# Keeping the split second expert matrix in a DRAM scratch between passes

## The chip, the cores and the metric

The kernel runs on one core of a Trainium2 chip. The metric is the device time of one execution, in microseconds (us). The kernel before takes 5032.78 us, the median of 3 runs (5029.45 to 5037.81).

## What is computed

The reference is two layers of a token mixer followed by an expert layer. The mixers and norms don't matter here. The expert layer does, cut to its core:

```python
def peer(h, wq, subkeys, u, v):
    # expert [t, heads, 16] and gate [t, heads, 16] come from a product-key search
    a = gelu(einsum('cd,chkd->chk', h, u[expert]))
    w = gate * a
    return einsum('chk,chkd->cd', w, v[expert])
```

There are 16384 experts of 1024 numbers each. Layer 0 works on 512 latent and 256 context tokens, layer 1 on the 512 latent ones. Everything is float32.

## The kernel before, in words

**Tiles and passes.** Tokens stand in tiles of 128. The second sum is computed as a dense product over all 16384 experts: a table `P` holds, for a pair of token tiles, the summed factor of each expert, and `vpass` (line 1027) multiplies it by the whole matrix `peer_v`. One call of `vpass` is a pass. Layer 0 has three passes, for the tile pairs (2,3), (4,5) and (0,1); layer 1 has two, for (2,3) and (0,1). So `peer_v` of a layer is read three times or twice.

**Columns.** A pass walks 128 columns `j`, in two halves of 64. Column `j` is the 128 x 1024 block of the experts `i*128 + j`, 512 KB. `load(jj)` (line 1033) fetches it on SP's queue (line 1042) into a float32 tile, ScalarE copies it into a float16 tile (line 1043), and the remainder is computed by VectorE (line 1045) or GpSimd (line 1047), so that `vh` holds a high and a low float16 part, again 512 KB. In the first pass of a layer a quarter of the remainders goes to VectorE, in the later passes half of them. TensorE then does 12 matmuls of 512 columns (line 1060). The tiles have names: the source is `s4` (three buffers) and `vh` is `hl` (three buffers), but each fourth column uses `h2Uh` and `h2Ul`, with one buffer each.

**What runs beside it.** During a half of a pass, `Scatter.step` (line 1147) builds the next table: per step four comparisons and products on VectorE (lines 1167 to 1170), 16 matmuls of 64 columns (lines 1172 and 1173) and copies back. The second half of the last pass of a layer has no such work. For tiles marked dense, `Scatter.at` (line 1108) multiplies the table by values from a spill (line 1120) and splits it (lines 147 and 149) for TensorE. For the tiles that are not dense, `gather` (line 908) fetches one row of the first expert matrix per token with an indirect DMA on GpSimd's queue (line 920, 512 KB) and multiplies it on VectorE (line 926), 128 times for each tile, through three buffers `r`. Layer 0 has three such tiles, layer 1 one. `Scatter.prep` (line 1131) of a tile that is not dense first issues what is left of its gather.

**What sets the order.** The program emits the work of a column, then a rate of background steps (`tick`, with `RATES`). A planner then orders the instructions of each engine by when it expects them to be ready, with the order of emission as priority; it may move work forward across columns and passes. The engines follow that order. One order is written by hand: `queue_behind` (line 901) places each gather on GpSimd's queue behind `self.lo_ins`, the most recent remainder that was given to GpSimd (line 1047 or 161).

Of the kernel before, what the change touches and what calls it, by code (L numbers as in the profile page):

```python
# [9 lines left out]
F16 = mybir.dt.float16  # L10
# [39 lines left out]
class Hybrid:  # L50
# [17 lines left out]
            for l in range(layers):  # L68
                self.layer(l, last=l == 1)

    # ---------------------------------------------------------------- constants
    def consts(self):
        nc, c, tmp = self.nc, self.cst, self.tmp
        dl = tmp.tile([128, 128], F32, name="dl")
# [37 lines left out]
                gens.pop(0)  # L112

    def tick(self, gens, rate):
        """Moves the generators on by rate on the average."""
        self.due = getattr(self, "due", {})
        k = id(gens)
        self.due[k] = self.due.get(k, 0.0) + rate
        n = int(self.due[k])
        self.due[k] -= n  # L120
        self.step(gens, n)
# [54 lines left out]
        nc.tensor.matmul(out, al, bh, start=False, stop=stop)  # L176


    # ---------------------------------------------------------------- modulation
    def srow(self, src, which, dst=None):  # L180
        dst = src if dst is None else dst
        self.nc.scalar.dma_start(src, self.i["cvec"][which].partition_broadcast(128))
# [28 lines left out]


    def vectors(self, l, last, pool, ps):
        """The factors that vary along a row, written out as rows."""
        nc = self.nc
        n = 4 if last else 8
        c = pool.tile([128, 8, KC], F32, name="vcol", bufs=1)
        md = self.modT[l]
        for w in range(n // 4):
            nc.vector.tensor_scalar(c[:, w * 4], md[2][:, :, w], 1.0 / WS, None, op0=OP.mult)  # L220
            nc.vector.scalar_tensor_tensor(c[:, w * 4 + 1], md[4][:, :, w], 1.0, self.g2[l], op0=OP.add, op1=OP.mult)
            nc.vector.tensor_copy(c[:, w * 4 + 2], md[3][:, :, w])
            nc.vector.tensor_scalar(c[:, w * 4 + 3], md[5][:, :, w], 1.0 / PS, None, op0=OP.mult)
        nc.tensor.transpose(ps[:n * KC, :128], c[:, :n].rearrange("p r k -> p (r k)"), self.idf)
        r = pool.tile([64, 128], F32, name="vrow", bufs=1)
        nc.scalar.activation(r[:n * KC], ps[:n * KC, :128], AF.Copy)
        self.vec = self.tc.dram_tile([n, D], F32, name=f"vec{l}")
        nc.sync.dma_start(self.vec.rearrange("r (k c) -> (r k) c", c=128), r[:n * KC])
# [3 lines left out]
        self.nc.sync.dma_start(r, self.vec[which * 4 + k].partition_broadcast(128))  # L232
        return r

    # ---------------------------------------------------------------- layer
    def load_x(self, tile_, t, eng=None, c=0):
        e = eng or self.nc.sync
        if self.res is None:
# [31 lines left out]
            self.res = self.nxt  # L270
            self.lo_ins = None

    # ---------------------------------------------------------------- mixers
    def mixers(self, l, last, wes):
        tiles = XTILES if last else XTILES + CTILES
        qkv_es = ExitStack()
# [197 lines left out]
        self.split(nat[:, 0], nat[:, 1], self.roped(pr, p, pool, "r", k, 4))  # L474
        self.to_stack(self.rtT, pr, 0 if k == "q" else 2, nat, ps)

    # ---------------------------------------------------------------- attention
    def probs_T(self, ap_, ps, e, nk):
        nc = self.nc
        tp = ps.tile([128, D], F32, name="w2", bufs=2)  # L480
# [166 lines left out]


    def strips(self, l, h, pool):
        """Decay by distance: forwards over positive, backwards over negative distances, both at zero."""  # L650
        nc = self.nc
        if h == 0:
            lg = self.lg = pool.tile([128, 8], F32, name="lg", bufs=1)
            nc.sync.dma_start(lg, self.i["decay"][l].partition_broadcast(128))
            nc.scalar.activation(lg, lg, AF.Exp, scale=-1.0)
            nc.scalar.activation(lg, lg, AF.Ln, bias=1.0)
            self.ng = pool.tile([128, 3, 8], F32, name="ng", bufs=1)
            for x, f in enumerate((-1.0, -256.0, -512.0)):
                nc.vector.tensor_scalar(self.ng[:, x], lg, f, None, op0=OP.mult)
            self.dd = pool.tile([128, 896], F32, name="dd", bufs=1)  # L660
            nc.gpsimd.iota(self.dd, pattern=[[1, 896]], base=-384, channel_multiplier=-1,
                           allow_small_or_imprecise_dtypes=True)
        dd, lg, ng = self.dd, self.lg, self.ng
        f, b = h, 4 + h
        s = pool.tile([128, 896], F32, name="strip")
        w = pool.tile([128, 896], F32, name="stript", bufs=1)
        nc.vector.tensor_scalar(s, dd, lg[:, f:f + 1], 0.0, op0=OP.mult, op1=OP.max)
        nc.vector.tensor_scalar(w, dd, ng[:, 0, b:b + 1], 0.0, op0=OP.mult, op1=OP.max)
        nc.vector.tensor_tensor(s, s, w, op=OP.add)
        nc.scalar.activation(s, s, AF.Exp, scale=-1.0)  # L670
        nc.vector.scalar_tensor_tensor(s, dd, 0.0, s, op0=OP.is_equal, op1=OP.add)
        c = pool.tile([128, 640], F32, name="stripc", bufs=1)
        nc.scalar.activation(c, dd[:, 256:896], AF.Exp, scale=ng[:, 0, f:f + 1], bias=ng[:, 1, f:f + 1])
        nc.scalar.activation(w[:, :640], dd[:, 256:896], AF.Exp, scale=lg[:, b:b + 1], bias=ng[:, 2, b:b + 1])
        nc.vector.tensor_tensor(c, c, w[:, :640], op=OP.add)
        return s, c


    # ---------------------------------------------------------------- output projection, second norm
    def wload(self, l, es, c):  # L680
        nc = self.nc
        pool = self.pool(es, f"wow{c}", 1, side="right")
# [74 lines left out]
        for t in order[len(order) - WLAG:]:  # L757
            second(t)

    # ---------------------------------------------------------------- product-key routing  # L760
    def routing(self, l, pool, ps, tiles, rp):
        nc = self.nc
        n = len(tiles)
# [133 lines left out]
        self.rt[t] = (st.rearrange("p a k h -> p a (k h)"), sg.rearrange("p k h -> p (k h)"), ix)  # L897


    # ---------------------------------------------------------------- gathered first expert matrix  # L900
    def queue_behind(self, ins):
        if self.lo_ins is not None:
            self.tc.add_manual_dep(ins.ins, self.lo_ins.ins.name,
# [29 lines left out]
        yield  # L933


    # ---------------------------------------------------------------- experts
    def need(self, t):
        while t not in self.done:
            self.step(self.bg, 1)
# [1 line left out]
    def peer(self, es, l, last, h2s):  # L941
# [30 lines left out]
        with ExitStack() as e:  # L972
            ps = self.pool(e, "ups", 4, space=PSUM)
            self.upass(l, 1, sc, ps, "pa", RATES[l][1], PRATE[l], more)
        self.accp = self.pool(es, "acc", 1, space=PSUM)
        for n, tiles in enumerate(self.groups):
            if n == 2:
                r = lambda: self.gp.tile([128, D], F32, name="r")
                vec = [self.srow(r(), 0, self.hpp.tile([128, D], F32, name="hp")), self.srow(r(), 1)]
                self.rg.append(self.ada(1, range(6), vec, r, lambda: self.sp.tile([128, D], F16, name="gst", bufs=GST)))  # L980
            follow = Scatter(self, self.groups[n + 1]) if n + 1 < len(self.groups) else None
            self.vpass(l, tiles, int(tiles[0] > 3), sc, follow, RATES[l][2 + 2 * n:4 + 2 * n])
            sc = follow
# [43 lines left out]
    def vpass(self, l, tiles, which, sc, follow, rates):  # L1027
# [3 lines left out]
        for half in range(2):  # L1031
            ahead = sc.step(1) if half == 0 else follow.step(0) if follow else iter(())
            def load(jj):
                j = half * 64 + jj
                ws = sc.at(half, jj)
                if j % 4 == 3:
                    v = self.lp.tile([128, 1536], F32, name="h2Uh")[:, :D]
                    vh = self.lp.tile([128, 3072], F16, name="h2Ul")[:, :2 * D].rearrange("p (z d) -> p z d", z=2)
                else:
                    v = self.vp.tile([128, D], F32, name="s4", bufs=3)  # L1040
                    vh = self.vp.tile([128, 2, D], F16, name="hl", bufs=3)
                nc.sync.dma_start(v, vr[:, j])
                nc.scalar.activation(vh[:, 0], v, AF.Copy)  # L1043
                if j % 4 in VDVE[sum(sc.dense)]:
                    nc.vector.tensor_tensor(vh[:, 1], v, vh[:, 0], op=OP.subtract)  # L1045
                else:
                    self.lo_ins = nc.gpsimd.tensor_tensor(vh[:, 1], v, vh[:, 0], op=OP.subtract)  # L1047
                return ws, vh

            vs = [load(jj) for jj in range(PF[1])]  # L1050
            for jj in range(64):
                j = half * 64 + jj
                if jj + PF[1] < 64:
                    vs.append(load(jj + PF[1]))
                ws, vh = vs.pop(0)
                for s in range(2):
                    a, b = ws[s]
                    for i, (w, x) in enumerate(((a, 0), (a, 1), (b, 0))):
                        for hf in range(2):
                            nc.tensor.matmul(acc[s][hf], w, vh[:, x, hf * 512:hf * 512 + 512],  # L1060
                                             start=j == 0 and i == 0, stop=j == 127 and i == 2)
                if jj % 2 == 1:
                    next(ahead, None)
                self.tick(self.rg, 0.4)
                self.tick(self.bg, rates[half])
# [22 lines left out]


class Scatter:  # L1090
    """Sums the gates of a pair of tiles into a table over all experts; over given values the sums are multiplied in."""

    def __init__(self, o, tiles, G=False):
        self.o, self.tiles, self.G = o, tiles, G
# [2 lines left out]
        self.sT = {}  # L1097

    def col(self, half, jj, n=1):
        """The table's columns jj.. of a half."""  # L1100
        w = 32 if half else 64
        p = self.P[half][jj // w]
        return p[:, :, jj % w:jj % w + n] if n > 1 else p[:, :, jj % w]
# [2 lines left out]
        return p[:, s].rearrange("p j t -> p (j t)").bitcast(F16).rearrange("p (z j t) -> p z j t", z=2, t=128)  # L1106

    def at(self, half, jj):
        """The stationary operands of expert column jj: a pair of parts for each token tile."""
        o, nc = self.o, self.o.nc  # L1110
        x, w = jj % 2, 32 if half else 64
        if any(self.dense) and x == 0:
# [143 lines left out]
```

## Time and profile before

| what | value |
| --- | --- |
| median of 3 runs | 5032.78 us |
| span of the profiled execution | 5040.9 us |
| first pass of layer 0 (first to last matmul) | 1469.2 to 1977.0 us |
| second pass of layer 0 | 1989.6 to 2505.2 us |
| third pass of layer 0 | 2517.2 to 2912.1 us |
| first pass of layer 1 | 4143.2 to 4613.2 us |
| second pass of layer 1 | 4630.7 to 5023.2 us |
| TensorE, VectorE, ScalarE, GpSimd busy | 90%, 72%, 44%, 44% of the span |

The profile is of one execution, whose span is 8.1 us (0.16%) above the median of the runs shown. Busy shares are averages over stages with different limits, so the passes are read one by one, in windows that begin at the first matmul of line 1060 of a half pass and end with its last.

### The profile page before, as it was taken

To read this page: it belongs to the slowest core of one execution; us is meant where nothing else is said; L and a number is where in the kernel's file an instruction comes from. 1 tells how busy PE (TensorE), PEld (TensorE's weight loads), DVE (VectorE), ACT (ScalarE), POOL (GpSimd) and SP (SyncE) were. 2 spreads that over 40 slices of the span, in tenths; PEclk is the share of its full clock that TensorE was granted. 3 is DMA by queue.
4 is the path that set the end of the run, shared out by engine and by line. 5 is a ranking of instruction groups with operands and counts; after the bars stand their busy time and mean duration, and the time that the engine had idled before them with its cause. 6 is when DMAs were issued, how large, how long until landed. Compare 5 with 4: busy or idle time off the path is not lost. (4 is left out here: it accounts for less than half of the span.)

```text
span 5040.9 us, 79837 instructions
## 1 busy us (share of the span) xinstructions
PE 4516.0 (90%) x30416; PEld 2857.2 (57%) x30416; DVE 3624.2 (72%) x7163; ACT 2209.1 (44%) x3694; POOL 2221.1 (44%) x1493
## 2 busy tenths in 40 slices
PE   4987888978999988998899999788878999998998
PEld 3664566745665554554555467455545766655553
DVE  7777549897889999988798245745775777667543
ACT  5556344343433343433334466644444443343443
POOL 4224133457566665555233422422456544443333
PEclk9996999989999998999899999799999999998999
DMA  5421446668777767877578632144657764445555
GB/s 180 150 65 35 156 134 208 194 196 282 249 255 251 247 245 256 290 256 277 188 235 270 202 122 66 39 145 134 208 183 251 249 222 149 143 151 166 168 188 176
DMA packets 379873, 955.15 MB, mean 189 GB/s; under 512 B 43632, under 2 KB 158800, under 8 KB 379488
## 3 DMA queue, kind: packets, MB, share of 16 engines
q1 hardware_dynamic: 296000, 675.74, 41.6%
q0 software_dynamic: 73888, 268.53, 15.0%
q10 hardware_dynamic: 9600, 5.77, 0.4%
q8 instruction: 238, 3.90, 0.3%
q14 instruction: 147, 1.20, 0.1%
HBM read 920.49 MB, written 29.41 MB: 188 GB/s over the span
## 5 line engine op out<-in xcount | busy, mean ns | idle before, releaser
L1047 POOL TENSOR_TENSOR hl<-s,hl 128x1024 f16<-128x1024 f32 x384 | 861.8, 2244 | 1077.0 <-ACT hl L1043 1075.1
L1060 PE MATMUL acc<-hl,gst 128*128 128x512 f16 x3456 | 835.4, 391 | 17.6 <-DVE gst L149 9.0
L926 DVE SCALAR_TENSOR_TENSOR r<-r,hp 128x1024 f32<-128x1024 f32 x512 | 619.4, 1213 | 284.0 <-DMA r<-peer_u,ix 283.1
L1043 ACT ACTIVATE hl<-s 128x1024 f16<-128x1024 f32 x480 | 505.2, 1057 | 697.7 <-PE acc L1060 313.5
L1060 PEld LDWEIGHTS <-gst 128*128 128x128 f16 x4608 | 463.9, 101 | 565.6 <-issue 58.5
L920 POOL DMA_INDIRECT r<-peer_u,ix x512 | 547.2, 1069 | 391.5 <-DVE r L926 193.1
L1172 PE MATMUL pw<-oh,oi 128*128 128x64 f16 x2560 | 640.1, 300 | 72.0 <-DVE oh L1169 70.7
L1173 PE MATMUL pw<-ol,oi 128*128 128x64 f16 x2560 | 639.9, 301 | 13.7 <-DVE ol L1170 13.5
L1060 PE MATMUL acc<-hl,P 128*128 128x512 f16 x2304 | 558.5, 389 | 5.2 <-POOL hl L1047 3.1
L1060 PEld LDWEIGHTS <-P 128*128 128x128 f16 x3072 | 307.8, 100 | 354.1 <-issue 27.7
L1172 PEld LDWEIGHTS <-oi 128*128 128x128 f16 x2560 | 372.5, 146 | 133.9 <-DVE oh L1169 74.0
L174 PE MATMUL pw<-h2Uh,hl 128*128 128x384 f16 x1024 | 352.4, 344 | 56.4 <-ACT gst L1017 56.2
L1169 DVE TENSOR_TENSOR oh<-oj,sT 128x512 f16<-128x512 f16 x320 | 257.8, 806 | 201.8 <-PE pw L1172 197.5
L161 POOL TENSOR_TENSOR hl<-s,hl 128x1024 f16<-128x1024 f32 x136 | 299.0, 2200 | 227.0 <-ACT hl L160 173.3
L1173 PEld LDWEIGHTS <-oi 128*128 128x128 f16 x2560 | 373.4, 146 | 18.5 <-issue 1.5
L176 PE MATMUL pw<-h2Uh,hl 128*128 128x384 f16 x1024 | 351.8, 344 | 25.1 <-DVE hl L151 18.9
L176 PE MATMUL pa<-h2Uh,hl 128*128 128x384 f16 x1024 | 341.8, 334 | 34.7 <-POOL hl L161 34.6
L175 PE MATMUL pw<-h2Ul,hl 128*128 128x384 f16 x1024 | 351.7, 343 | 0.0
L174 PE MATMUL pa<-h2Uh,hl 128*128 128x384 f16 x1024 | 342.6, 335 | 1.5 <-ACT hl L160 1.5
L175 PE MATMUL pa<-h2Ul,hl 128*128 128x384 f16 x1024 | 341.1, 333 | 0.0
L176 PEld LDWEIGHTS <-hl 128*128 128x128 f16 x2048 | 207.0, 101 | 214.3 <-POOL hl L161 50.2
L1045 DVE TENSOR_TENSOR h2Ul<-h2Uh,h2Ul 128x1024 f16<-128x1024 f32 x160 | 233.6, 1460 | 130.3 <-ACT h2Ul L1043 130.3
(297 smaller groups left out, 9801.1 us busy)
## 6 DMA issues: line engine op xcount, KB each, us to landing
s<-peer_v SPq DMA_DIRECT2D x480, 512.0 KB
s<-ut SPq DMA_DIRECT2D x256, 512.0 KB
h2Uh<-peer_v SPq DMA_DIRECT2D x160, 512.0 KB
wq<-peer_wq SPq DMA_DIRECT2D x128, 256.0 KB
wst<-w_in SPq DMA_DIRECT2D x96, 256.0 KB
r<-w_ada SPq DMA_DIRECT2D x48, 512.0 KB
h2T<-w_ada SPq DMA_DIRECT2D x32, 512.0 KB
spill<-gst SPq DMA_DIRECT2D x64, 256.0 KB
```

The lines of the kernel that those rows point to most:

```text
L161: self.lo_ins = nc.gpsimd.tensor_tensor(lo, w, hi, op=OP.subtract)
L174: nc.tensor.matmul(out, ah, bh, start=start, stop=False)
L175: nc.tensor.matmul(out, ah, bl, start=False, stop=False)
L176: nc.tensor.matmul(out, al, bh, start=False, stop=stop)
L920: self.queue_behind(nc.gpsimd.indirect_dma_start(out=r, out_offset=None, in_=self.i["peer_u"], in_offset=bass.IndirectOffsetOnAxis(ap=ix[: ...
L926: nc.vector.scalar_tensor_tensor(r, r, 1.0, hp, op0=OP.mult, op1=OP.mult, accum_out=a[:, k - AHEAD:k - AHEAD + 1])
L1043: nc.scalar.activation(vh[:, 0], v, AF.Copy)
L1047: self.lo_ins = nc.gpsimd.tensor_tensor(vh[:, 1], v, vh[:, 0], op=OP.subtract)
L1060: nc.tensor.matmul(acc[s][hf], w, vh[:, x, hf * 512:hf * 512 + 512], start=j == 0 and i == 0, stop=j == 127 and i == 2)
L1169: nc.vector.tensor_tensor(oh, oj, col[2].to_broadcast([128, 64, TB]), op=OP.mult)
L1172: nc.tensor.matmul(pp[:, t0 - tb + x], oi[:, :, x], oh[:, :, x], start=True, stop=False)
L1173: nc.tensor.matmul(pp[:, t0 - tb + x], oi[:, :, x], ol[:, :, x], start=False, stop=True)
```

## The change

In the first pass of a layer each column's `vh` is stored to a DRAM scratch `vsplit`, on SP's queue, after the column's matmuls were emitted. In the later passes `load` fetches that block into a tile and does nothing else. These passes load three columns ahead of the matmuls in the order of emission instead of one, and use `s4`, `hl`, `h2Ul` and `h2Uh` as tiles for what they load. Comments that the diff also drops are left out here.

```diff
@@ peer
         self.accp = self.pool(es, "acc", 1, space=PSUM)
+        self.vsplit = self.tc.dram_tile([128, 128, 2, D], F16, name=f"vsplit{l}")
         for n, tiles in enumerate(self.groups):
+            self.first = n == 0
@@ vpass
             def load(jj):
                 j = half * 64 + jj
                 ws = sc.at(half, jj)
+                if not self.first:
+                    if j % 4 == 3:
+                        vh = self.lp.tile([128, 3072], F16, name="h2Ul" if j % 8 == 3 else "h2Uh")[:, :2 * D]
+                    else:
+                        vh = self.vp.tile([128, 2 * D], F16, name="s4" if j % 4 == 1 else "hl", bufs=3)
+                    vh = vh.rearrange("p (z d) -> p z d", z=2)
+                    nc.sync.dma_start(vh, self.vsplit[j])
+                    return ws, vh
...
-            vs = [load(jj) for jj in range(PF[1])]
+            pf = PF[1] if self.first else 3
+            vs = [load(jj) for jj in range(pf)]
             for jj in range(64):
                 j = half * 64 + jj
-                if jj + PF[1] < 64:
-                    vs.append(load(jj + PF[1]))
+                if jj + pf < 64:
+                    vs.append(load(jj + pf))
                 ws, vh = vs.pop(0)
...
+                if self.first:
+                    nc.sync.dma_start(self.vsplit[j], vh)
                 if jj % 2 == 1:
                     next(ahead, None)
```

## Rows read from the trace of the kernel before

**Rows 1.** Costliest groups of the page: busy us, mean ns | idle before, releaser.

```profile
L1047 POOL TENSOR_TENSOR hl<-s,hl 128x1024 f16<-128x1024 f32 x384 | 861.8, 2244 | 1077.0 <-ACT hl L1043 1075.1
...
L1043 ACT ACTIVATE hl<-s 128x1024 f16<-128x1024 f32 x480 | 505.2, 1057 | 697.7 <-PE acc L1060 313.5
...
L1045 DVE TENSOR_TENSOR h2Ul<-h2Uh,h2Ul 128x1024 f16<-128x1024 f32 x160 | 233.6, 1460 | 130.3 <-ACT h2Ul L1043 130.3
```

**Rows 2.** Windows: stretch, length, PE, PEld, DVE, ACT, POOL busy, PEclk, DMA share, GB/s.

```profile
1469.20:1709.70 240.50, 233.60 (x1250) 136.77 (x1251) 236.29 (x329) 83.83 (x95) 167.40 (x98) 0.97 0.70 244
1716.40:1977.00 260.60, 238.52 (x1269) 138.92 (x1270) 245.94 (x325) 99.92 (x127) 159.41 (x99) 0.95 0.70 241
1989.60:2228.70 239.10, 232.47 (x1233) 134.84 (x1233) 214.57 (x344) 94.17 (x156) 133.81 (x92) 0.96 0.82 283
2230.40:2505.20 274.80, 244.61 (x1274) 140.14 (x1273) 215.96 (x362) 96.76 (x129) 120.08 (x78) 0.91 0.67 230
2517.20:2744.40 227.20, 224.98 (x1234) 133.50 (x1234) 219.04 (x331) 83.07 (x125) 79.95 (x34) 0.99 0.77 258
2746.10:2912.10 166.00, 166.00 (x772) 75.43 (x771) 45.71 (x51) 67.90 (x72) 64.93 (x32) 1.00 0.65 204
4143.20:4369.50 226.30, 226.30 (x1250) 135.29 (x1251) 158.92 (x230) 83.81 (x95) 105.08 (x48) 0.99 0.47 149
4372.80:4613.20 240.40, 232.65 (x1269) 137.96 (x1270) 160.56 (x235) 99.24 (x125) 99.65 (x45) 0.98 0.48 154
4630.70:4855.50 224.80, 224.80 (x1218) 131.74 (x1219) 120.60 (x238) 98.10 (x152) 76.88 (x33) 0.97 0.54 173
4857.30:5023.20 165.90, 165.90 (x770) 75.05 (x767) 49.62 (x66) 73.36 (x92) 63.82 (x30) 1.00 0.63 197
```

**Rows 3.** Groups by line, second pass of layer 0 (1989 to 2505 us).

```profile
L926 DVE SCALAR_TENSOR_TENSOR r<-r,hp 128x1024 f32<-128x1024 f32 x105 | 127.3, 1213 | 62.2 <-DMA r<-peer_u,ix 62.0
```

**Rows 4.** Waits, 2230 to 2505 us: who waited for whom, us, times, longest.

```profile
DVE r L926 <- DMA r<-peer_u,ix: 38.3, 19, 4.8
...
PE acc L1060 <- DVE gst L149: 9.0, 2, 5.9
```

**Rows 5.** Windows of three other stretches, columns as in rows 2.

```profile
1139.00:1220.00 81.00, 61.70 (x343) 36.87 (x342) 64.42 (x95) 28.17 (x47) 56.64 (x43) 0.89 0.86 285
2380.00:2410.00 30.00, 23.44 (x96) 9.95 (x96) 19.25 (x32) 9.75 (x12) 16.96 (x13) 0.89 0.92 320
...
1469.00:1977.00 508.00, 474.34 (x2536) 277.72 (x2537) 485.90 (x662) 186.17 (x226) 329.46 (x199) 0.95 0.70 245
```

**Rows 6.** DMA of the first pass of layer 0 (1469 to 1977 us).

```profile
DMA packets 35448, 124.27 MB, mean 245 GB/s; under 512 B 3937, under 2 KB 5601, under 8 KB 35414
```

**Rows 7.** DMA of the first pass of layer 1 (4143 to 4613 us).

```profile
DMA packets 22917, 71.16 MB, mean 151 GB/s; under 512 B 2545, under 2 KB 6641, under 8 KB 22886
```

**Rows 8.** Groups by line, 1139 to 1220 us, where gathers stand closest.

```profile
L926 DVE SCALAR_TENSOR_TENSOR r<-r,hp 128x1024 f32<-128x1024 f32 x30 | 36.3, 1215 | 16.7 <-DMA r<-peer_u,ix 16.6
```

**Rows 9.** Groups by line, 2384 to 2422 us, the rest of a gather in a row.

```profile
L926 DVE SCALAR_TENSOR_TENSOR r<-r,hp 128x1024 f32<-128x1024 f32 x13 | 15.8, 1217 | 14.0 <-DMA r<-peer_u,ix 13.9
```

**Rows 10.** Line 1120: duration ns min/median/max, first and last start us.

```profile
L1120 DVE TENSOR_TENSOR P<-P,gsp x128: 407/416/2375, 1851.3 to 4850.0; 128x256 f32<-128x256 f32 x128
```

**Rows 11.** Line 1043: its engine sat idle before it (us, times) until.

```profile
  PE acc L1060: 484.6, 311
...
  DMA s<-peer_v: 47.6, 19
```

**Rows 12.** SP's waits in the first pass of layer 0.

```profile
SPq L1042 <- DVE h2Ul L1045: 244.5, 32, 12.2
```

**Rows 13.** Timeline between the first and second pass of layer 0: start us, us, instruction.

```profile
1983.66 0.33 SPq L1042 DMA_DIRECT2D s<-peer_v  x1
...
1988.51 1.06 ACT L1043 ACTIVATE hl<-s 128x1024 f16<-128x1024 f32 x1 [6.62 <-DMA s<-peer_v]
...
1989.62 1.01 PE L1060 MATMUL acc<-hl,P 128*128 128x512 f16 x2 [0.96 <-ACT hl L1043]
```

## The prediction, made before the changed kernel was run

> **What bounds the kernel now.** I cut the trace into the ten half passes and read clock, engines and DMA of each [rows 2]. Two kinds of half pass are at TensorE's floor. The halves without table work take 166.0 and 165.9 us, TensorE busy throughout at a granted clock of 1.00 (the 2.4 GHz level). Three halves with table work take 227.2, 226.3 and 224.8 us, TensorE busy for 99% or more. I take 226 us as the floor of a half with table work. Above it stand five halves: 240.5 and 260.6 (first pass, layer 0), 239.1 and 274.8 (second pass, layer 0) and 240.4 (layer 1, first pass, second half).
>
> So of the six halves that stop splitting, four are at the floor already: 227.2, 166.0, 224.8, 165.9. What the change can win stands in the second pass of layer 0: 13.1 + 48.8 = 62 us, and at the seams between passes. The causes there are to be seen in the waits: VectorE sits 62.0 us of that pass waiting for gathered rows [rows 3], 38.3 of them in its second half, where TensorE in turn waits for VectorE's split of the table [rows 4].
>
> **Removed work.** Three later passes of 128 columns lose 384 copies on ScalarE at 1.06 us (407 us), 192 remainders on GpSimd at 2.24 us (430 us) and 192 on VectorE at 1.46 us (280 us) [rows 1]. In the four halves at the floor all of that lies beside TensorE, and I cost it at nothing. In the second pass of layer 0, VectorE loses 64 x 1.46 = 93 of its 431 busy us [rows 1, 2]. If only that mattered, its halves would go to about 230 and 237 us. The second value lies between the floor and the 240.4 us of layer 1's first pass, which has the same preparations, no gathers and some splits [rows 2]. That would be 47 us won.
>
> **What the removal takes with it.** The gathers are paced by hand: each stands on GpSimd's queue behind the newest remainder. In the later passes there is none any more, so from the second pass of layer 0 on they stand behind one that is long past. The planner does move work far ahead: line 1120 of the second pass, which begins at 1989.6, first runs at 1851.3 [rows 10]. Hence I expect all 105 gathers of this pass [rows 3] to be planned as early as VectorE has room. VectorE's other work there is 431 - 127 for the gathers' multiplies - 93 = 211 us, or 105 a half [rows 1 to 3]. Within 226 us that leaves 121 us, room for 121 / 1.21 = 100 multiplies: nearly all would be planned into the first half.
>
> The chip can't follow that plan. Three buffers turn over at the pace of DMA, VectorE and GpSimd together. Where gathers stand closest now, 30 take 81 us, 2.7 us each, with VectorE waiting 16.6 us for rows to land, DMA at 0.86 and TensorE busy for 62 of 81 us [rows 5, 8]. VectorE works in order, so scatter steps and table splits queue up behind a row that is late, and TensorE waits for those. I take 105 x 2.7 = 284 us for the first half and 237 for the second: 521 against 513.9, so **+7 us**. The ends: 230 + 237 = 467 (-47) if the plan stays as loose as now, and 105 x 38 / 13 = 307, with 237 together 544 (+30), at the pace of the 13 gathers between 2384 and 2422 us [rows 9].
>
> **Added stores.** Each first pass gets 128 stores of 0.524 MB, 67.1 MB. On SP that is 128 issues at about 0.33 us, taken from a load [rows 13]: 42 us in a pass of 508, on a queue that spends 244.5 us waiting for one kind of remainder alone [rows 12]. A store waits for both parts of its column. Behind it on SP stand later loads; these wait for the same remainders, which free their source tiles, so the added wait costs nothing. If a store stood ahead of a load that is already free, the cover would be the time that ScalarE waits for TensorE to release `hl`, 484.6 us against 47.6 for loads from `peer_v` [rows 11]. The `hl` tile is now also released by its store; TensorE reads it some columns after the split, so I cost that at nothing too.
>
> What counts is DMA traffic. The first pass of layer 0 moves 124.27 MB in 508 us at a share of 0.70 [rows 5, 6]: 508 x 0.70 / 124.27 = 2.86 us per MB. In the fullest stretch, 30 us at 0.92 and 320 GB/s, it is 27.6 us / 9.6 MB = 2.88 [rows 5]. So 124.27 + 67.1 = 191.4 MB would need 191.4 x 2.87 = 549 us: **+41** as the upper end. The lower end is 0: a share contains packets that wait on an otherwise idle engine, and no row shows the path full. VectorE is busy for 486 of these 508 us [rows 5], and each gather that lands later adds to it. I take the middle, **+20**. A gain I exclude for the stores: they take nothing away.
>
> The Trainium skill, page "DMA: Bandwidth & Descriptors", section "Specifications", puts the limit of HBM at about 358 GB/s for each core: by that 191.4 MB take 535 us, +27, and the sum below would be 7 us higher. Its section "Measured" has 425 GB/s for one core that streams alone in large transfers, by which they take 450 us and hide. No row here shows more than 320 GB/s over 30 us.
>
> The first pass of layer 1 moves 71.16 MB [rows 7]; with 67.1 more it is 138.3 x 2.87 = 397 us of 470, a share of 0.84. The nearest row is the 239.1 us half at 0.82, 13 above the floor, but with gathers [rows 2]. Ends 0 and +13 for each half; with no gathers there I take **+3** in all.
>
> **Seams.** Between the passes TensorE does no line 1060 work for 12.6, 12.0 and 17.5 us [rows 2]. In the first of these the next load is issued at 1983.66, its split begins at 1988.51 and the first matmul follows at 1989.62 [rows 13]. Now the first block goes into an `hl` tile that frees before the sums are written out, and needs no split. But sums must leave PSUM and the table be finished, and some table work fills these gaps already. Ends 0 (the first load waits for the last store) and -25 for the three; I take **-10**.
>
> **Sum.** 20 + 3 + 7 - 10 = +20 us. The profiled span of 5040.9 is 8.1 us above the median of the runs; I add the difference to the median: 5032.8 + 20 = **5053 us**.
>
> **The rivals.**
> 1. *The gathers keep their place and VectorE is relieved.* The second pass falls by 47, the seams by 10, and the stores cost 12 and 2: 5032.8 - 43 = 4990 us. For it: 93 us of VectorE work go, and all of the 62 us above the floor sit where VectorE is late. Against it: nothing holds the gathers. It decides if their spacing in the first half of the second pass stays near what it is over the pass now, 516 / 105 = 4.9 us [rows 3]; the break-even of that pass is 2.64 us of forced spacing.
> 2. *The stores hide.* DMA at 0.70 still has idle time, and loads have cover [rows 11]. Then only +7 and -10 are left: 5030 us, no change that shows. The page's 425 GB/s is this case, and the trace neither shows nor excludes it.
> 3. *Both presses combine.* DMA is full in the first pass (+41), layer 1 loses 13, and gathers, slowed by DMA that is already at 0.82 in that half, take 2.9 us (+30), with no seam won: +84, 5117 us.
>
> That the splits would not vanish I exclude, since `load` returns before them.
>
> **How the numbers follow.** Forecast (5042 to 5085) 0.42; rival 1 0.33; rival 2 0.16; rival 3 0.09. About 0.2% (10 us) is what a measurement of this kernel can tell from no change. Faster is rival 1, 0.33; same is rival 2, 0.16; slower is the rest, 0.51. The range goes down to 4977, past rival 1 by the rest of the seams, and up to 5108, a little short of rival 3. As both signs hold much of the chance: the likeliest case's own range is 5042 to 5085.
>
> **What would show it.** In the windows of the changed kernel: the four halves at the floor unchanged within 2 us; both halves of the first pass of layer 0 longer, at a DMA share of 0.9 or more; the first half of the second pass at 260 to 300 us, its 105 gathers mostly in it, with VectorE waiting for gathered rows by far more than the 62 us of now; the second half near 237. I am wrong if gathers stay spread over both halves, or if the first pass keeps its 508 us at a DMA rate near 377 GB/s.

## The result and the profile after

The changed kernel takes 5153.55 us (median of 4 runs, 5147.91 to 5158.63), the kernel before 5031.11 (4 runs). The ratio is 1.0237, 95% interval 1.0223 to 1.0250: 122 us slower. The forecast had the sign, but 5053 us, and a range that ended at 5108. The profiled span went from 5040.9 to 5147.3 us, by 106.4; the medians moved by 122, since the profiled execution of before was longer than all of its timed runs (5037.8 at most) and that of the changed kernel was one of its shorter ones.

These are the windows of the changed kernel for the ten half passes, with the columns and in the order of [rows 2]. The line of the matmuls is now 1071.

```profile
1462.10:1766.90 304.80, 254.90 (x1268) 142.71 (x1269) 239.48 (x338) 85.58 (x97) 161.28 (x96) 0.89 0.84 302
1766.70:2088.50 321.80, 261.93 (x1286) 145.12 (x1285) 237.73 (x314) 102.05 (x129) 165.77 (x106) 0.87 0.85 302
2088.30:2344.00 255.70, 238.37 (x1266) 137.87 (x1265) 193.62 (x408) 31.94 (x93) 83.29 (x85) 0.95 0.95 346
2345.80:2589.50 243.70, 230.35 (x1274) 137.63 (x1272) 127.42 (x269) 36.20 (x70) 16.37 (x17) 0.97 0.59 198
2591.30:2825.60 234.30, 230.77 (x1268) 137.68 (x1266) 146.47 (x312) 24.42 (x63) 0.00 (x0) 0.97 0.73 255
2827.30:2993.30 166.00, 166.00 (x772) 75.43 (x771) 5.41 (x20) 5.02 (x12) 1.11 (x2) 1.00 0.61 199
4223.00:4458.30 235.30, 231.85 (x1268) 138.11 (x1269) 171.88 (x236) 84.80 (x96) 102.43 (x46) 0.98 0.78 271
4458.10:4728.90 270.80, 254.81 (x1302) 145.48 (x1301) 170.26 (x207) 101.81 (x130) 111.82 (x48) 0.91 0.70 249
4737.20:4961.90 224.70, 221.04 (x1203) 128.89 (x1202) 97.23 (x238) 34.41 (x90) 0.66 (x1) 0.98 0.62 199
4963.60:5129.60 166.00, 165.99 (x770) 75.03 (x768) 14.64 (x34) 12.86 (x31) 0.00 (x0) 1.00 0.59 193
```

Against [rows 2], first to last matmul of each pass:

| stretch | before, us | after, us | difference |
| --- | --- | --- | --- |
| layer 0, first pass | 507.8 | 626.4 | +118.6 |
| layer 0, second pass | 515.6 | 501.2 | -14.4 |
| layer 0, third pass | 394.9 | 402.0 | +7.1 |
| layer 1, first pass | 470.0 | 505.9 | +35.9 |
| layer 1, second pass | 392.5 | 392.4 | -0.1 |
| three seams | 42.1 | 9.9 | -32.2 |
| all else | | | -8.5 |

The whole loss, 154.5 us, stands in the two first passes, the only ones that store. The later passes and the seams give back 40. In the first pass of layer 0 TensorE also gets a lower granted clock, 0.89 and 0.87 of 2.4 GHz in the mean over the two levels instead of 0.97 and 0.95.

What the first pass of layer 0 waits for now (waits of 1462 to 2088 us; who waited for whom, us in total, times, longest):

```profile
DVE r L926 <- DMA r<-peer_u,ix: 130.4, 63, 6.9
ACT hl L1053 <- DMA s<-peer_v: 93.3, 51, 4.5
PE acc L1071 <- DVE h2Ul L1055: 90.0, 27, 6.7
```

In the kernel before, ScalarE hardly waited for these loads (same view, 1469 to 1977 us):

```profile
ACT h2Ul L1043 <- DMA h2Uh<-peer_v: 36.4, 10, 5.0
...
ACT hl L1043 <- DMA s<-peer_v: 1.7, 1, 1.7
```

SP's own waits in that stretch of the changed kernel show who is late before them. Line 1074 is the store:

```profile
SPq L1074 <- DVE h2Ul L1055: 237.8, 28, 12.7
SPq L1074 <- POOL hl L1057: 203.0, 74, 6.0
```

SP used to wait in its loads, for tiles to come free [rows 12]. Now it waits in its stores, and the loads stand behind them. One turn of this, in order of time (start us, us, instruction):

```profile
1575.09 1.06 ACT L1053 ACTIVATE h2Ul<-h2Uh 128x1024 f16<-128x1024 f32 x1 [8.62 <-DMA h2Uh<-peer_v]
...
1581.06 1.22 DVE L926 SCALAR_TENSOR_TENSOR r<-r,hp 128x1024 f32<-128x1024 f32 x1 [2.51 <-DMA r<-peer_u,ix]
...
1582.87 1.68 DVE L1055 TENSOR_TENSOR h2Ul<-h2Uh,h2Ul 128x1024 f16<-128x1024 f32 x1
...
1584.58 0.33 SPq L1074 DMA_DIRECT2D vsplit<-h2Ul  x1
1584.61 4.42 PE L1071 MATMUL acc<-h2Ul,gst 128*128 128x512 f16 x10 [6.72 <-DVE h2Ul L1055]
...
1585.01 2.88 SPq L1074 DMA_DIRECT2D vsplit<-hl  x2
...
1587.94 0.47 SPq L1052 DMA_DIRECT2D h2Uh<-peer_v  x1
```

Column 27 is copied at 1575.09. Its remainder on VectorE comes only at 1582.87, since VectorE stands at a gathered row that comes late: its buffer was free at 1561.24, but its gather was issued only at 1572.04, behind a remainder on GpSimd, and landed 9 us later. The store of column 27 waits for that remainder, and TensorE with it, 6.72 us. Then SP holds two more stores, the second of which waits until 1587.6 for column 29. Only then comes the load of column 31, though its source tile `h2Uh` has been free since 1584.55. It is copied at 1594.3, and the turn begins anew: four columns take some 20 us (626.4 / 32) instead of 16 in the kernel before (507.8 / 32).

### The profile page after: what moved, and what is told of

The parts are those of the page before. It is cut to its first block, busy times and chain, and to the rows that moved or that the text cites. A ratio compares the mean times of both kernels' runs of the same rounds, so it can differ in the third digit from the quotient of the medians.

```text
span 5147.3 us, 78956 instructions
## 1 busy us (share of the span) xinstructions
PE 4560.6 (89%) x30416; PEld 2865.1 (56%) x30416; DVE 3318.5 (64%) x6971; ACT 1827.6 (36%) x3310; POOL 1786.6 (35%) x1301
## 5 line engine op out<-in xcount | busy, mean ns | idle before, releaser
L1071 PE MATMUL acc<-hl,gst 128*128 128x512 f16 x3072 | 733.4, 388 | 24.7 <-POOL hl L1057 21.5
L1057 POOL TENSOR_TENSOR hl<-s,hl 128x1024 f16<-128x1024 f32 x192 | 433.0, 2263 | 559.9 <-ACT hl L1053 558.9
L147 ACT ACTIVATE gst<-P 128x512 f16<-128x512 f32 (+1 forms) x256 | 133.4, 523 | 807.3 <-PE acc L1071 754.8
L149 DVE TENSOR_TENSOR gst<-P,gst 128x512 f16<-128x512 f32 (+1 forms) x256 | 190.4, 745 | 323.3 <-ACT gst L147 323.2
L1071 PE MATMUL acc<-hl,P 128*128 128x512 f16 x1536 | 373.2, 386 | 13.3 <-DVE P L1196 6.7
L161 POOL TENSOR_TENSOR hl<-s,hl 128x1024 f16<-128x1024 f32 x136 | 303.4, 2233 | 224.1 <-ACT hl L160 167.4
L176 PE MATMUL pa<-h2Uh,hl 128*128 128x384 f16 x1024 | 341.4, 334 | 35.9 <-POOL hl L161 35.8
L1071 PE MATMUL acc<-h2Ul,gst 128*128 128x512 f16 x960 | 288.1, 450 | 95.8 <-DVE h2Ul L1055 91.2
L168 POOL TENSOR_TENSOR rstd<-rstd,mhalf 128x1 f32<-128x1 f32 x26 | 15.7, 604 | 998.1 <-DVE rstd L167 989.4
```

The source lines that it names most:

```text
L147: nc.scalar.activation(hi, src, AF.Copy, scale=scale)
L149: (lo_eng or nc.vector).tensor_tensor(lo, src, hi, op=OP.subtract)
L161: self.lo_ins = nc.gpsimd.tensor_tensor(lo, w, hi, op=OP.subtract)
```

## The experiments

Ten kernels were run, most with one timed execution beside one of the kernel before (5036.0 us for the first four, 5028.8 for the next four, a median of 5029.7 for the last two). Those runs of the kernel before lie between 5021 and 5037 us, so two single runs that differ by less than some 16 us are not told apart. **Queue theory**: the loss is that loads stand behind stores on SP. **Traffic theory**: the loss is the 67.1 MB more in each first pass, which make loads and gathers land later. Windows below are of the first pass of layer 0 (507.8 us before, 626.4 after), unless said otherwise, with the columns of [rows 2].

### The stores alone

```diff
+        self.vsplit = self.tc.dram_tile([128, 128, 2, D], F16, name=f"vsplit{l}")
...
+                if self.first:
+                    nc.sync.dma_start(self.vsplit[j], vh)
```

> The kernel before with the 256 stores of the changed kernel and nothing else of it: the later passes load and split as before, the scratch is never read. Both theories: the first passes lengthen as in the changed kernel (508 to about 626 us in layer 0, 470 to about 506 in layer 1), the total goes to about 5031 + 155 = 5186 us, and the later passes stay within 5 us of the kernel before. A third theory, that the first passes lengthened through another plan of the whole program rather than through the stores, expects them shorter than 560 and 485 us.

Measured: 5182.0 us, 146 above before; layer 1's first pass 506.7 us.

```profile
1467.00:2089.30 622.30, 516.10 (x2551) 287.66 (x2552) 477.94 (x651) 187.61 (x226) 325.30 (x199) 0.88 0.84 304
```

The stores make the whole loss, 115 and 37 us in the first passes, and put the loads and stores on SP in the same order as in the changed kernel. What the rest of the change wins is the difference to the changed kernel, some 25 to 30 us.

### The waits without the bytes

```diff
+                if self.first:
+                    nc.sync.dma_start(self.vsplit[j][:, :, 960:], vh[:, :, 960:])
```

> As the run with stores only, but each store moves the last 64 of 1024 numbers of both parts, a sixteenth of the bytes (4.2 MB a pass), with the same waits on SP; the scratch isn't read and stays incomplete. Queue theory (a store waits on SP for the split of its column, and the loads behind it wait with it): first passes still about 590 us or more and 495 us or more, total above 5130 us. Traffic theory (67 MB more in each first pass make loads and gathers land later): first passes within 15 us of 508 and 470, total 5031 to 5065 us.

Measured: 5038.3 us, 2 above before; layer 1's first pass 471.5 us.

```profile
1472.00:1984.70 512.70, 477.39 (x2536) 278.53 (x2537) 482.86 (x657) 185.13 (x225) 331.42 (x199) 0.95 0.75 250
```

That is what the traffic theory has. But the planner, for which a thin store is short, had also put the stores elsewhere: the store of column j now stood between the loads of columns j+3 and j+4. So this run had neither the bytes nor the bad order.

### The bytes without the waits, first try

```diff
+                if self.first:
+                    for z in range(2):
+                        nc.sync.dma_start(self.vsplit[j][:, z], self.iox.rearrange("p a b -> p (a b)"))
```

> As the run with stores only, but what is stored is a constant table (two stores of 256 KB for each column, the same 67.1 MB a pass), so that no store waits for a split; the scratch holds no split block and isn't read. Queue theory: first passes at most 25 us above 508 and 10 above 470, total 5031 to 5070 us. Traffic theory: about 626 and 506 us, total about 5186 us.

Measured: 5056.8 us. It looks like the queue theory and says nothing for it: with nothing to wait for, the planner sent all stores ahead, those of layer 1 too, into the first 1000 us of the program. The stretch up to the first pass of this kernel, 28 us longer than in the kernel before, and the pass itself:

```profile
0.00:1497.00 1497.00, 1229.49 (x10079) 855.28 (x10079) 1112.49 (x2743) 688.57 (x1327) 616.78 (x490) 0.92 0.76 260
1497.60:2008.60 511.00, 475.82 (x2536) 277.73 (x2537) 489.97 (x662) 185.99 (x225) 327.41 (x199) 0.95 0.70 243
```

### The changed kernel with another order on SP

```diff
                 if self.first:
-                    nc.sync.dma_start(self.vsplit[j], vh)
+                    held.append((j, vh))
+                    if j >= 3:
+                        k, old = held.pop(0)
+                        put(k, old, self.ld.get(k + 4))
```

Here `put` issues the store with an order on SP's queue, not a wait, behind the load that it is given.

> The changed kernel with one thing more: the store of column j is put on SP's queue behind the load of column j+4, which waits for the same remainder. All bytes and all waits stay, but no load stands behind a store whose column is later than the load's own source tile needs. Queue theory: the first passes fall to about 530 and 475 us, the total from 5153 to about 5020 us, below the kernel before. Traffic theory: the first passes stay within 20 us of 626 and 506, the total above 5120 us.

Measured: 5100.4 us, 53 below the changed kernel and 64 above before; layer 1's first pass 491.2 us, which contains some table work of the next half (113 more matmuls).

```profile
1469.50:2039.60 570.10, 501.50 (x2631) 292.21 (x2632) 478.35 (x669) 186.73 (x236) 321.23 (x200) 0.94 0.91 327
```

Both theories missed. The order is worth 56 us of this pass; the other 62 stay. The pass now also contains more table work than the changed kernel's, 1095 of its matmuls instead of 1015. The waits of ScalarE moved: it no longer waits for loads, but for the stores to release the `hl` and `h2Ul` tiles.

```profile
ACT hl L1053 <- DMA vsplit<-hl: 61.0, 30, 4.1
...
ACT h2Ul L1053 <- DMA vsplit<-h2Ul: 39.8, 12, 7.4
```

### The bytes in the pass, without waits and held tiles

```diff
+                for z in range(2):
+                    self.st[j] = nc.sync.dma_start(self.vsplit[j][:, z], self.iox.rearrange("p a b -> p (a b)"))
+                    behind(self.st[j], self.ld.get(j + 3), "store behind load")
...
+                behind(self.ld[j], self.st.get(j - 4), "load behind store")
```

> The kernel before with constant stores again (the scratch holds no split block and isn't read), 67.1 MB a pass, but now each is put on SP's queue between the loads of columns j+3 and j+4, so that the bytes move during the first pass and nothing waits for a split or holds an hl tile. Traffic alone: if bytes are what costs, the first pass of layer 0 takes 560 us or more and that of layer 1 about 490; if queue order and held tiles are what cost, 508 to 535 and 470 to 476 us. My forecast: 525 and 472, total about 5055 us.

Measured: 5114.1 us, 85 above before; layer 1's first pass 493.7 us, with 114 matmuls of the next half in it.

```profile
1469.70:2040.80 571.10, 500.12 (x2630) 292.43 (x2630) 503.16 (x667) 182.52 (x236) 318.87 (x199) 0.94 0.93 330
```

My forecast of 525 us was wrong. No store waits here and none holds a tile of the split, and the pass takes 571 us, as with the right order, at a DMA share of 0.93.

But these 63 us are not shown to be the cost of the bytes alone, since the planner ordered the other engines differently too. The pass took in table work from the seam and the next pass, 94 matmuls more than before (lines 1172 and 1173 of that kernel); TensorE's busy time for that work rose from 133.6 to 158.0 us. And ScalarE's copies now stand behind the splits of the table (line 147), where ScalarE waits for TensorE. For loads it no longer waits, and VectorE waits for rows by 24 us more than the 14.0 of before:

```profile
ACT gst L147 <- PE acc L1076: 260.4, 55, 10.8
...
DVE r L926 <- DMA r<-peer_u,ix: 37.9, 41, 3.0
...
ACT hl L1059 <- DMA s<-peer_v: 0.5, 1, 0.5
```

The kernel before had, in the same pass:

```profile
ACT gst L147 <- PE acc L1060: 6.0, 1, 6.0
```

No run moved all the bytes with the order of before on ScalarE and TensorE. What a DMA path this full costs by itself stays open.

### The thin stores' order with all bytes

The edit is that of the run before, made to the changed kernel, with the split block in place of the constant:

```diff
-                for z in range(2):
-                    self.st[j] = nc.sync.dma_start(self.vsplit[j][:, z], self.iox.rearrange("p a b -> p (a b)"))
+                self.st[j] = nc.sync.dma_start(self.vsplit[j], vh)
                 behind(self.st[j], self.ld.get(j + 3), "store behind load")
```

> The changed kernel with a fixed order on SP's queue: load of column j+3, store of column j, load of column j+4, which is the order that the run with thin stores had by itself. All bytes, waits and held tiles stay as in the changed kernel. If the order is the main cause, the first passes fall from 626 and 506 us to about 540 and 478, and the run beats the order of the run before (571 and 491), because the store goes ahead of a load that has time and so gives its tile back sooner. If held tiles and traffic are the main cause, they stay at about 571 and 491. Total about 5035 or 5100 us.

Measured: 5103.0 us, 74 above before; layer 1's first pass 491.8 us.

```profile
1468.80:2049.20 580.40, 505.92 (x2631) 294.10 (x2632) 493.97 (x671) 182.68 (x236) 319.64 (x200) 0.93 0.90 325
```

Giving tiles back sooner brings nothing: either good order ends at 570 to 580 us, where the constant stores end too. This run shares their plan as well: 1095 table matmuls in the pass, and ScalarE waits at line 147 for 260.5 us.

### Gathers paced again

```diff
                     nc.sync.dma_start(vh, self.vsplit[j])
+                    if j % 4 not in VDVE[sum(sc.dense)]:
+                        pc = self.sp.tile([128, 1], F16, name="pace")
+                        self.lo_ins = nc.gpsimd.tensor_tensor(pc, vh[:, 0, 0:1], vh[:, 1, 0:1], op=OP.add)
```

> The changed kernel, and in its later passes a one-column addition on GpSimd at each column where the kernel before had its remainder there, for the gathers to stand behind. The first passes stay as in the changed kernel (626 and 506 us). If the loss of pace is what keeps the second pass of layer 0 at 501 us, its halves go from 255.7 and 243.7 to about 232 and 240 us, and the total falls by 20 to 30 us, to about 5128. Rival: the gathers bring the same rows in either order and the pass stays within 8 us of 501.

Measured: 5150.9 us. The second pass of layer 0:

```profile
2095.70:2339.80 244.10, 235.32 (x1266) 138.15 (x1265) 163.91 (x363) 33.48 (x93) 65.16 (x91) 0.96 0.87 311
2341.50:2603.40 261.90, 233.88 (x1274) 138.19 (x1273) 154.20 (x313) 36.10 (x70) 52.56 (x78) 0.94 0.66 232
```

The time moved from one half to the other, as the theory has it, but the sum is 506 against 499 us without pace. The rival was right: with these first passes, the loss of pace costs nothing.

The next run has this edit on top of the thin stores' order with all bytes.

> The fixed order on SP and the paced gathers together. If the two are separate causes, their effects add: about 5035 - 25 = 5010 us, below the kernel before. If one eats the other (gathers that come later meet the same full DMA path), no more than 10 us below the run with the fixed order alone.

Measured: 5101.4 us, 1.6 below the fixed order alone, which single runs don't tell apart. It is the same finding.

### Half of the scratch

```diff
+                if not self.first and j % 2 == 0:
+                    vh = self.vp.tile([128, 2, D], F16, name="hl", bufs=3)
+                    nc.sync.dma_start(vh, self.vsplit[j])
+                    return ws, vh
...
-                if j % 4 in VDVE[sum(sc.dense)]:
+                if self.first and j % 4 in VDVE[sum(sc.dense)]:
```

Even columns alone are stored, in the order of the run with all bytes; the later passes load one column ahead, as before. They also give all the remainders that are left to GpSimd, where the kernel before gave half of them to VectorE.

> Half of the change: only the even columns go through the scratch (33.6 MB more in each first pass), in the fixed order on SP; the later passes load these and split the odd ones, all remainders on GpSimd, so that VectorE is relieved as in the changed kernel and the gathers keep their pace. If full DMA is what is left of the cost when the order is right, 157.8 MB at the 2.82 us per MB that the run with in-pass constant stores showed is 445 us of DMA, below the 508 us of the pass: the first passes take 508 to 525 and 470 to 480 us, the second pass of layer 0 480 to 500 us, and the total 4995 to 5025 us, faster than the kernel before. If the cost is one of each store and not of a full path, the first pass of layer 0 takes about 508 + 35 = 543 us and the total is 5035 us or more.

Measured: 5010.64 us (median of 5) against 5029.69 (median of 8); ratio 0.9962, interval 0.9948 to 0.9976. It is 19 us faster than the kernel before. The first pass of layer 0 and the halves of the second:

```profile
1467.80:1985.20 517.40, 479.29 (x2536) 278.66 (x2537) 481.22 (x657) 185.86 (x225) 331.13 (x199) 0.94 0.86 307
1991.20:2226.20 235.00, 229.82 (x1252) 135.56 (x1251) 198.58 (x346) 62.41 (x125) 127.59 (x90) 0.98 0.86 307
2228.80:2491.70 262.90, 238.12 (x1272) 138.91 (x1272) 184.62 (x314) 65.57 (x101) 111.14 (x77) 0.94 0.66 235
```

Half of the bytes cost 10 us and not half of 63. That would fit a cost that begins only where the path is nearly full, but ScalarE's order and the table work in the pass are those of before here, so it may as well be the plan. Layer 1's first pass takes 464 us, a little less than forecast, and the second pass of layer 0 500.5 us. What wins is mostly the seams: 6.0, 1.8 and 3.7 us instead of 12.6, 12.0 and 17.5, of which some 12 come back as longer passes behind the last two. No run moved the remainders to GpSimd alone, so how much of the gain is the scratch's is not shown.

### The changed kernel's order without the bytes

```diff
+                    st = nc.sync.dma_start(self.vsplit[j][:, :, 960:], vh[:, :, 960:])
+                    if j % 4 == 2 and self.ld.get(j + 1) is not None:
+                        behind(st, self.ld[j + 1])
...
+                if self.first and j % 4 in (0, 3) and j - 2 in self.st:
+                    behind(self.ld[j], self.st[j - 2])
```

> Thin stores (a sixteenth of the bytes; scratch incomplete and not read) in the order that the changed kernel has on SP: loads of columns 4k+3 and 4k+4 to 4k+6 stand behind the stores of columns two earlier. Order alone: if a load that stands behind a later store is what costs, the first pass of layer 0 takes 560 us or more and that of layer 1 490 or more. If order costs only together with the long landing of full stores, loads and gathers, they take at most 525 and 476 us, total 5030 to 5055. My forecast is the second, with 520 us.

Measured: 5050.4 us, 21 above before; layer 1's first pass 469.0 us.

```profile
1470.50:1990.70 520.20, 475.40 (x2535) 277.35 (x2536) 473.84 (x653) 182.25 (x225) 317.70 (x199) 0.95 0.74 246
```

This order is a little stricter than the changed kernel's: the load of column 4k+6 also stands behind the store of 4k+3 here. Even so it costs 12 us of this pass, 8 more than the thin stores in their own order. But its cover is gone: ScalarE waits for loads all the time, with some 250 us in sum where it was 38 in the kernel before.

```profile
ACT h2Ul L1055 <- DMA h2Uh<-peer_v: 145.6, 25, 9.1
ACT hl L1055 <- DMA s<-peer_v: 107.9, 62, 6.0
```

## Why the prediction was wrong

**What the runs say together**, for the first pass of layer 0: order without the bytes +12 (520.2), bytes in a good order +62 to +73 (570.1 to 580.4), both +115 (622.3). The order takes little by itself, and 42 to 52 us once the bytes are there.

The way to this goes through GpSimd, where each gather stands behind a remainder. A late load makes a late copy, a late remainder and then a late gather. These are waits of the kernel before (1469 to 1977 us):

```profile
POOL hl L1047 <- ACT hl L1043: 99.1, 44, 15.3
...
POOL r L920 <- DVE r L926: 57.8, 26, 3.9
...
DVE r L926 <- DMA r<-peer_u,ix: 14.0, 10, 5.0
```

In the changed kernel (1462 to 2088 us) GpSimd waits for copies, and far less for a buffer of a gather to come free:

```profile
POOL hl L1057 <- ACT hl L1053: 256.8, 51, 13.3
...
POOL r L920 <- DVE r L926: 25.2, 12, 3.8
```

In the median over the pass, a gather was issued 2.6 us after its buffer came free in the kernel before, 7.9 us after it in the changed kernel. In the run with the blocked order and thin stores it was 6.8 us, and VectorE waited only 37.6 us for rows, against 130.4 with all bytes: here late gathers cost little as long as they landed soon. VectorE was the busiest engine of this pass before, with 486 busy us and 14 of waiting for rows in 508; its wait for rows grew by 116 us, and the pass by 119. No run took the pacing out of the first pass.

That loads and rows do land later is in the DMA view: median us from issue to landing in the changed kernel's first pass of layer 0, last number,

```profile
s<-peer_v SPq DMA_DIRECT2D x90, 512.0 KB, 8.9
...
r<-peer_u,ix POOLq DMA_INDIRECT x108, 8.3
```

and in the run with thin stores, in the same pass:

```profile
s<-peer_v SPq DMA_DIRECT2D x90, 512.0 KB, 6.8
...
r<-peer_u,ix POOLq DMA_INDIRECT x106, 6.5
```

Point by point:

- **The step that failed** is that of the added wait on SP: "these wait for the same remainders, which free their source tiles, so the added wait costs nothing". It holds for a store of column j ahead of the load of column j+4. The planner put the stores of two later columns ahead of a load that was already free. I named the cover for that case, ScalarE's 484.6 us of waiting for TensorE, and took it as enough. That is a sum over the whole program; in the first pass of layer 0 it was 108 us (79.8 for `hl`, 27.8 for `h2Ul`). The order used it up, as the run without the bytes shows, and the wait that I put at nothing is worth 53 us of the total: that is what the changed kernel wins with another order on SP. I also had the pacing of the gathers only as something that goes in the later passes, and not as what hands a late load on to VectorE in the first.
- **The bytes were sized too low, as far as the runs can tell.** I had 0 to +41 and took +20; with the order put right, 62 to 73 us are left, and constant stores make 63. How much of that is DMA and how much the other plan, with its 24 us of table work, is open. The price of 2.87 us per MB held (571 x 0.93 / 188 MB = 2.82). But the pass ended at a share of 0.93 in that run, and at 0.84 and 0.85 in the changed kernel, where I had forecast 0.9 or more. The Trainium skill, page "DMA: Bandwidth & Descriptors", section "Specifications", has about 358 GB/s for a core, by which 191.4 MB would take an estimated 535 us; the trace shows 330 GB/s over this pass and at most 346 over a half pass, so it was nearer than the 425 of its section "Measured".
- **Layer 1's first pass**: +3 forecast, +36 measured, at a DMA share of 0.74 and with no gathers. With a good order it takes 491 us, with the next half's table work in it, and that next half is 13 to 15 us shorter than before. Both passes of layer 1 with their seam take 880 us before, 907 in the changed kernel and 883 or 885 with a good order. So with the bytes in place the order is nearly the whole loss there; without them it costs nothing (469.0 us).
- **The second pass of layer 0**: +7 forecast, -14.4 measured. The gathers did run ahead: 86 of 106 stand in the first half now, against 57 before, 3.0 us each. These are the multiplies of the two halves in the changed kernel:

```profile
L926 DVE SCALAR_TENSOR_TENSOR r<-r,hp 128x1024 f32<-128x1024 f32 x86 | 104.2, 1216 | 55.0 <-DMA r<-peer_u,ix 54.8
...
L926 DVE SCALAR_TENSOR_TENSOR r<-r,hp 128x1024 f32<-128x1024 f32 x20 | 24.4, 1218 | 16.3 <-DMA r<-peer_u,ix 16.2
```

  But the first half took 255.7 us and not 284. I let TensorE wait until all rows were done; in fact a fifth of them went on in the second half. That paced gathers are no better (506 us) says that nothing was lost by the pace. Nor was much won: in the runs whose later passes are those of the kernel before, this pass took 502 to 508 us from first to last matmul, so most of the 14 us isn't owed to the work removed. No run came below 500, and my first rival's 467 was not in reach; VectorE still waits 71 us for rows, hardly more than the 62 of before, where I had expected far more.
- **Right**: three of the four halves at the floor (166.0, 224.7, 166.0 within 0.1 us; the fourth takes 234.3 instead of 227.2, since 32 matmuls of table work moved into it from the seam before it), the excluded gain of removed work there, and the direction of the seams, which gave 32 us and not 10, more than the end of 25.
- **Luck**: the third rival's 5117 us came nearest, but it had 30 us of loss in the second pass of layer 0, which got shorter, and no gain at the seams.

What stays open is how the 62 us that neither good order on SP removed divide between a nearly full DMA path and the planner's other order on ScalarE and TensorE; no run separated these.

## What to carry to other kernels

A store that waits for a result stands in the same queue as the loads for later work, and if a load that could already go stands behind it, the wait may cost more than its length: read the queue's order and its waits before trusting the cover. Look also for what else is ordered behind the late work, as the gathers are here. Trading computation for DRAM traffic did not pay in full here: the whole scratch lost 2.4%, or 1.3 to 1.5% with a good order, while half of it, with its remainders on GpSimd, won 0.4%. Work taken off engines that are already beside the bound wins nothing; of the six relieved halves three didn't move and two grew. And an experiment that changes the size of a transfer can change the order of every engine: compare the orders before calling the difference traffic.

## What was not expected of the hardware

The same order on SP cost 12 us without the bytes and 42 to 52 us with them, in a pass of 508. And a queue's order can change with the size of the transfers alone, since the planner goes by their length; the run with thin stores and the one with stores of a constant each measured another order than intended. In the first pass of layer 0 of the changed kernel the granted clock fell, from 0.97 and 0.95 to 0.89 and 0.87, as TensorE came to wait more, and its busy time for the pass rose from 472 to 517 us for nearly the same count of instructions.
